# Inverse of the 16x16 blocks by columns' contributions, and two scale-and-shift steps on ScalarE, in a one-core RWKV and HGRN kernel

## Chip, cores and metric

The kernel runs on one core of a Trainium2 chip. The metric is the time of one execution in microseconds, measured on the device; before the change it is 2753.27 us (median of three runs). TensorE multiplies, VectorE and ScalarE do the element-wise work, POOL (GpSimd) and SP (SyncE) here mostly start transfers.

## The reference, cut to what matters

Two transformer blocks over 256 tokens of width 2048. The change lies in the first, in the RWKV-7 recurrence of 32 heads of 64 (`h` for a head, state 64x64):

```python
w = -softplus(-(w0 + tanh(xw @ w1) @ w2)) - 0.5
decay = exp(-exp(w))
a = sigmoid(a0 + (xa @ a1) @ a2)
kk = heads(k * k_k); kk = kk * rsqrt(max(sum(kk * kk), 1e-24))
k = k * (1 + (a - 1) * k_a)
# for each token t, with a_vec = -kk, b_vec = kk * a:
sa = state @ a_t
state = state * w_t + sa b_t^T + v_t k_t^T
y_t = state @ r_t
```

## The kernel before

The recurrence is computed by chunks of 64 tokens. Inside a chunk the tokens depend on each other through a triangular 64x64 matrix, of which the kernel needs the inverse. It inverts the sixteen-wide diagonal blocks on VectorE and joins them with matmuls on TensorE (`s2`, levels `lev16` and `lev32`).

`jit` walks over eight groups of four heads. For each group TensorE makes the products k and v with float32 weights that are split into two parts, `hi` by ScalarE (L183) and `lo` by VectorE (L184), so that each product is three matmuls (`feat_p`, L1043 to L1045). Between these matmuls pieces of three generators are placed by hand: `s0` of the group itself (operands of the recurrence), `s1` of the group before (scores, inverse, transposes) and `s2` of the one before that (joining, the chain over four chunks, output norm). The lists `SLOT0`, `SLOT1`, `SLOT2` give the step j, 0 to 63 (one step for every three matmuls), from which a piece may be issued. Nothing reorders instructions afterwards: each engine takes its own in the order in which the code issues them, and waits where an operand is not ready. A fourth stream, `s3`, multiplies blocks of another weight (`ab<-in_adat`, 512 KB each) on VectorE at L507; it has one buffer, so that SP starts the next transfer only when L507 has read the last, and SP's queue has the weight transfers (`raw`) behind it. After the eighth group `wo` makes the output product, with the last group's `s1` and `s2` beside it; it needs `yhl`, splits of the recurrence's result by ScalarE (L287) and VectorE (L288).

The lines that the change and the prediction touch:

- `s0`, second piece: `sw` is the tanh of the decay's logit (tile `zw`). L1064 turns it into the sigmoid (0.5 x + 0.5); L1067 scans it into C (two instructions); ScalarE makes exp of it twice (L1068, L1070), and the square of `kkr` (L1076). TensorE sums the squares (L1079).
- `s0`, fourth piece: VectorE bounds the sum (L1080), ScalarE makes its inverse root by Ln and Exp (L1082, L1083), VectorE makes (ta - 1) * 0.5 k_a into `kb` from the tanh `ta` (tile `za`), half a group at a time (L1087), then (that + 1) * k (L1090). Later pieces: L1093, L1094, L1099 (into C again) and L1104.
- `s1`: TensorE's L1127 needs C of L1099; L1141 needs `LA` (L1118, L1119) and `kb`. POOL writes the scores `Aa` to device memory and loads the diagonal blocks as `G`, [64, 16, 16]: 64 blocks, one a partition. L1170 to L1182 are the inverse; five `yield`s cut it into six pieces. Then POOL stores P and its transpose and reloads them as `Pm`, `Tm`.
- `s2`: for each chunk c, TensorE makes `ch` (L1246), ScalarE copies it to `U` (L1249), TensorE multiplies by P (L1253), ScalarE copies to `VA`, `VB` (L1261), TensorE updates the state (L1266), ScalarE scales it (L1271), TensorE adds to the output `yT` (L1275).

`half` holds 0.5 w0, 0.5 a0 and 0.5 k_a, made once at L907.

Of the kernel before, what the change touches and what calls it, by code (L numbers as in the profile page):

```python
# [13 lines left out]
AF = mybir.ActivationFunctionType  # L14
ALU = mybir.AluOpType
AX = mybir.AxisListType
# [81 lines left out]
class Kern:  # L98
# [790 lines left out]
    def scan_pools(self, st):  # L889
        tc, nc = self.tc, self.nc  # L890
        self.sp = st.enter_context(tc.tile_pool(name="sc", bufs=1))
        z = self.T([64, 8, 64], "Tm")
        nc.vector.memset(z[:], 0.0)
        self.img = {}
        for i in range(2):
            for n in "PT":
                t = self.img[n, i] = self.dr.tile([1, 8 * CQ], F32, name=f"img{n}{i}")
                for hd in range(2):
                    nc.sync.dma_start(out=self.rows(t, hd), in_=z[:])
        self.Ep = self.T([128, 8, 65], "Ep")  # L900
        nc.vector.memset(self.Ep[:, :, 0:1], 1.0)
        self.scanm = self.sp.tile([128, 256], BF16, name="scanm")
        nc.vector.memset(self.scanm[:], 1.0)
        nc.vector.memset(self.scanm[:, 0:256:64], 0.0)
        self.half = self.T([128, 3, 16], "half")
        for i, n in enumerate(("w0", "a0", "k_a")):
            nc.vector.tensor_scalar(out=self.half[:, i, :], in0=self.v(n, 0, 16), scalar1=0.5, scalar2=None,  # L907
                                    op0=ALU.mult)

    def rows(self, t, hd):  # L910

# [6 lines left out]
    def T(self, shape, tag, bufs=1):  # L918
        return self.sp.tile(list(shape), F32, tag=tag, bufs=bufs, name=tag)
# [130 lines left out]
    def s0(self, g):  # L1050
        nc, f = self.nc, self.gr[g]
        T = self.T
        at = iter(self.SLOT0)
        c8 = lambda t: t.rearrange("p f (c t) -> p (f c) t", c=4)
        fl = lambda t: t.rearrange("p f t -> p (f t)")
        bc = lambda v: v.unsqueeze(2).broadcast_to([128, 2, S])
        vec2 = lambda n: self.v(n, 2 * g, 2)
        yield next(at)
        while self.kdone < g - 1:
            assert self.step("s1")  # L1060
        Ep = self.Ep
        sw, ta = f["w"], f["a"]

        nc.vector.tensor_scalar(out=sw, in0=sw, scalar1=0.5, scalar2=0.5, op0=ALU.mult, op1=ALU.add)  # L1064
        C = T([128, 2, S], "C")
        for i in range(2):
            nc.vector.tensor_tensor_scan(C[:, i, :], self.scanm[:], sw[:, i, :], 0.0, op0=ALU.mult, op1=ALU.add)  # L1067
        nc.scalar.activation(out=Ep[:, :, 1:65], in_=c8(C[:]), func=AF.Exp, scale=-KAPPA)  # L1068
        Em = sw
        nc.scalar.activation(out=Em, in_=C, func=AF.Exp, scale=KAPPA)  # L1070
        yield next(at)

        kkr = f["kkr"] = T([128, 2, S], "kkr")
        nc.vector.tensor_tensor(out=kkr, in0=f["k"], in1=bc(vec2("k_k")), op=ALU.mult)
        rn = rk = f["rk"] = C
        nc.scalar.activation(out=C, in_=kkr, func=AF.Square)  # L1076
        yield next(at)
        p = self.misc((128, 2, S))
        nc.tensor.matmul(fl(p[:]), lhsT=self.c("bones"), rhs=fl(C[:]), start=True, stop=True)  # L1079
        nc.vector.tensor_scalar(out=rn, in0=p[:], scalar1=1e-24, scalar2=None, op0=ALU.max)  # L1080
        self.lnset()
        nc.scalar.activation(out=rn, in_=rn, func=AF.Ln, scale=65536.0)  # L1082
        nc.scalar.activation(out=rn, in_=rn, func=AF.Exp, scale=-0.5, bias=self.b8)  # L1083

        kb = f["kb"] = T([128, 8, 128], "kb")
        for i in range(2):
            nc.vector.tensor_scalar(out=kb[:, i * 4:i * 4 + 4, 64:128],  # L1087
                                    in0=ta[:, i, :].rearrange("p (c t) -> p c t", c=4), scalar1=-1.0,
                                    scalar2=self.half[:, 2, 2 * g + i:2 * g + i + 1], op0=ALU.add, op1=ALU.mult)
        nc.vector.scalar_tensor_tensor(out=kb[:, :, 64:128], in0=kb[:, :, 64:128], scalar=1.0, in1=c8(f["k"][:]),  # L1090
                                       op0=ALU.add, op1=ALU.mult)
        yield next(at)
        nc.vector.tensor_tensor(out=kkr, in0=rn, in1=kkr, op=ALU.mult)  # L1093
        nc.vector.scalar_tensor_tensor(out=kb[:, :, 0:64], in0=c8(ta[:]), scalar=1.0, in1=c8(kkr[:]), op0=ALU.add,  # L1094
                                       op1=ALU.mult)
        yield next(at)
        r = self.r[:, 2 * g:2 * g + 2, :]
        for i in range(2):
            nc.vector.scalar_tensor_tensor(out=rk[:, i, :].rearrange("p (c t) -> p c t", c=4),  # L1099
                                           in0=r[:, i, :].rearrange("p (c t) -> p c t", c=4),  # L1100
                                           scalar=self.v("r_k", 2 * g + i), in1=kb[:, i * 4:i * 4 + 4, 64:128],
                                           op0=ALU.mult, op1=ALU.mult)
        kb4 = kb[:].rearrange("p c (j t) -> p c j t", j=2)
        nc.vector.tensor_tensor(out=kb4, in0=kb4, in1=c8(Em[:]).unsqueeze(2).broadcast_to([128, 8, 2, 64]),  # L1104
                                op=ALU.mult)
        yield next(at)

    def s1(self, g):
        nc, f = self.nc, self.gr[g]
# [4 lines left out]
        Ep, kb, kkr = self.Ep, f["kb"], f["kkr"]  # L1114
# [5 lines left out]
                                       op0=ALU.mult, op1=ALU.mult)  # L1120
# [5 lines left out]
        p = self.misc((128, 2, S))  # L1126
# [7 lines left out]
        for i in range(2):  # L1134
            for hd, L in ((0, LA), (1, LB)):
# [3 lines left out]
                p = self.misc((128, 4, 128))  # L1139
                for c in range(4):  # L1140
# [5 lines left out]
                                        op=ALU.mult)  # L1146
                nc.vector.tensor_tensor(out=L[os, cs, :], in0=p[64:128], in1=mb(slice(64, 128), slice(0, 128)),
                                        op=ALU.mult)
# [7 lines left out]
        for i in range(2):  # L1156
            cs = slice(i * 4, i * 4 + 4)
            p = self.misc((128, 4, 128))
# [7 lines left out]
        G = T([64, 16, 16], "G")  # L1166
# [3 lines left out]
        P = T([64, 16, 16], "PG")  # L1170
        tmp = T([64, 256], "tG")
        nc.vector.memset(P[:], 0.0)
        nc.vector.memset(P[:].rearrange("p a b -> p (a b)")[:, 0:256:17], 1.0)
        for t in range(1, 16):
            tv = tmp[:, 0:t * t].rearrange("p (a b) -> p a b", a=t)
            nc.vector.tensor_tensor(out=tv, in0=P[:, 0:t, 0:t], in1=G[:, 0:t, t].unsqueeze(1).broadcast_to([64, t, t]),
                                    op=ALU.mult)
            nc.vector.tensor_reduce(out=P[:, 0:t, t], in_=tv, axis=AX.X, op=ALU.add)
            if t in (4, 7, 9, 11, 13):
                yield next(at)  # L1180
        Tt = T([64, 16, 16], "tG")
        nc.vector.tensor_copy(out=Tt, in_=P[:].rearrange("p a b -> p b a"))  # L1182
# [12 lines left out]
        p = self.misc((128, 2, 2, 128))  # L1195
# [710 lines left out]
```

## Time and profile before

| | us |
|---|---|
| median of 3 runs (2752.15 to 2753.98) | 2753.27 |
| the profiled execution's own time | 2759.31 |
| its span, first to last instruction | 2757.5 |
| TensorE busy | 2608.1 (95%) |
| VectorE busy | 1775.8 (64%) |
| ScalarE busy | 1346.5 (49%) |
| the change's stage, `jit` and `wo` | about 221 to 790 of the span |

The profile is of one execution, whose time is 6 us above the median. Busy TensorE is the sum of its matmuls' times; the ends of pipelined matmuls are modelled. L12 is line 12 of the kernel; a row names an engine, a line, the tile written and the tiles read. Wait rows say which engine waited for whose result. Times in the timeline count from the start of the span.

### The profile page before, as it was taken

The numbers are of one execution on the slowest core, as the hardware profiler recorded it, in microseconds if no ns is written. First come the engines' busy times: TensorE is split into PE (matmuls) and PEld (weight loads), VectorE is DVE, ScalarE is ACT, GpSimd is POOL, SyncE is SP. The second block draws the span as 40 slices with busy tenths as digits, with TensorE's granted clock in tenths as the row PEclk, the third lists the DMA queues.
The fourth block names the chain that finished last, engine by engine and source line by source line (L and its number), as shares of the span: only waits on it lengthen the run. The fifth ranks groups of instructions, "written<-read, shape, count | busy, mean of one in ns | idle before, by whom it ended". The sixth has DMA issues, their size and how long they took to land.

```text
span 2757.5 us, 47818 instructions
## 1 busy us (share of the span) xinstructions
PE 2608.1 (95%) x19345; PEld 2377.1 (86%) x19345; DVE 1775.8 (64%) x2845; ACT 1346.5 (49%) x2206; POOL 61.6 (2%) x101
## 2 busy tenths in 40 slices
PE   6997999998879999999999989999989999999998
PEld 5997788886559999999888789998789999988887
DVE  5977888887567786666555556665554444555555
ACT  3245565664355444444444555655454444444444
POOL 0000111110000000000000000000000000000000
PEclk8999999999889999999999999999999999999999
DMA  8946555556656775555555544443535555556555
GB/s 326 389 145 200 191 191 185 192 182 205 223 193 240 271 268 187 183 183 184 176 194 194 176 155 145 139 139 122 192 131 184 183 183 183 183 191 194 195 192 159
DMA packets 151516, 534.13 MB, mean 194 GB/s; under 512 B 21376, under 2 KB 21760, under 8 KB 150272
## 3 DMA queue, kind: packets, MB, share of 16 engines
q1 hardware_dynamic: 146640, 515.36, 55.7%
q0 software_dynamic: 4368, 13.64, 1.9%
q8 instruction: 151, 2.47, 0.4%
q10 hardware_dynamic: 288, 2.10, 0.2%
q14 instruction: 69, 0.57, 0.1%
HBM read 524.73 MB, written 6.29 MB: 193 GB/s over the span
## 4 chain that ended last, share of the span: by engine, by line
PE 82%; DVE 6%; ACT 6%; DMA 5%; issue 2%; SPq 0%; DVEq 0%; ACTq 0%; POOLq 0%
PE ta L353 7%; PE ta L354 7%; PE ta L352 7%; PE f L276 6%; PE f L274 6%; PE f L275 6%; PE u L276 4%; PE u L275 4%; PE u L274 4%; PE m L1043 3%; PE m L1044 3%; PE m L1045 3%; DMA scratch<-in_adat 2%; PE r L776 2%; DVE spl L184 1%
## 5 line engine op out<-in xcount | busy, mean ns | idle before, releaser
L184 DVE TENSOR_TENSOR spl<-raw,spl 128x1024 fp32r<-128x1024 f32 x748 | 913.1, 1221 | 778.0 <-ACT spl L183 773.6
L183 ACT CAST spl<-raw 128x1024 fp32r<-128x1024 f32 x748 | 782.0, 1046 | 856.8 <-PE ta L354 307.2
L276 PE MATMUL f<-yhl,spl 128*128 128x256 f32 x1376 | 389.5, 283 | 0.4 <-DVE spl L184 0.4
L274 PE MATMUL f<-yhl,spl 128*128 128x256 f32 x1376 | 389.8, 283 | 0.0
L275 PE MATMUL f<-yhl,spl 128*128 128x256 f32 x1376 | 389.4, 283 | 0.0
L352 PE MATMUL ta<-spl,shl 128*128 128x512 f32 x832 | 324.6, 390 | 3.4 <-ACT shl L287 3.4
L353 PE MATMUL ta<-spl,shl 128*128 128x512 f32 x832 | 324.5, 390 | 1.5 <-DVE spl L184 1.5
L354 PE MATMUL ta<-spl,shl 128*128 128x512 f32 x832 | 324.4, 390 | 0.0
L274 PE MATMUL u<-hl,spl 128*128 128x256 f32 x1024 | 289.9, 283 | 0.0
L276 PE MATMUL u<-hl,spl 128*128 128x256 f32 x1024 | 289.8, 283 | 0.0
L275 PE MATMUL u<-hl,spl 128*128 128x256 f32 x1024 | 289.8, 283 | 0.0
L276 PEld LDWEIGHTS f<-yhl,spl 128*128 128x128 f32 x1376 | 264.2, 192 | 0.6 <-DVE spl L184 0.6
L275 PEld LDWEIGHTS f<-yhl,spl 128*128 128x128 f32 x1376 | 264.2, 192 | 0.0
L274 PEld LDWEIGHTS f<-yhl,spl 128*128 128x128 f32 x1376 | 264.2, 192 | 0.0
L1043 PE MATMUL m<-hl,spl 128*128 128x256 f32 x672 | 199.6, 297 | 0.0
L274 PEld LDWEIGHTS u<-hl,spl 128*128 128x128 f32 x1024 | 196.6, 192 | 0.0
L275 PEld LDWEIGHTS u<-hl,spl 128*128 128x128 f32 x1024 | 196.6, 192 | 0.0
L276 PEld LDWEIGHTS u<-hl,spl 128*128 128x128 f32 x1024 | 196.6, 192 | 0.0
L1044 PE MATMUL m<-hl,spl 128*128 128x256 f32 x672 | 189.9, 283 | 0.0
L1045 PE MATMUL m<-hl,spl 128*128 128x256 f32 x672 | 189.8, 282 | 0.0
L352 PEld LDWEIGHTS ta<-spl,shl 128*128 128x128 f32 x832 | 156.6, 188 | 36.6 <-ACT shl L287 3.8
L353 PEld LDWEIGHTS ta<-spl,shl 128*128 128x128 f32 x832 | 156.6, 188 | 34.5 <-DVE spl L184 2.1
(422 smaller groups left out, 4809.8 us busy)
## 6 DMA issues: line engine op xcount, KB each, us to landing
raw<-in_ffn_in SPq DMA_DIRECT2D x172, 512.0 KB, 4.7
raw<-in_w_up SPq DMA_DIRECT2D x128, 512.0 KB, 3.7
raw<-in_w_down SPq DMA_DIRECT2D x128, 512.0 KB, 4.0
raw<-in_ffn_out SPq DMA_DIRECT2D x86, 512.0 KB, 3.8
raw<-in_w_in SPq DMA_DIRECT2D x84, 512.0 KB, 3.7
raw<-in_w_rkv SPq DMA_DIRECT2D x76, 512.0 KB, 4.5
scratch<-in_adat SPq DMA_DIRECT2D x66, 512.0 KB, 5.9
ada<-in_ada SPq DMA_DIRECT2D x64, 512.0 KB, 6.7
```

Source lines behind the costliest of these rows:

```text
L183: self.nc.scalar.copy(out=hi[:, :n], in_=t[:, :n])
L184: self.nc.vector.tensor_tensor(out=lo[:, :n], in0=t[:, :n], in1=hi[:, :n].bitcast(F32), op=ALU.subtract)
L274: nc.tensor.matmul(out, lhsT=hi[:, w], rhs=xhl[:, 0, kc, :], start=(kc == 0), stop=False)
L275: nc.tensor.matmul(out, lhsT=hi[:, w], rhs=xhl[:, 1, kc, :], start=False, stop=False)
L276: nc.tensor.matmul(out, lhsT=lo[:, w], rhs=xhl[:, 0, kc, :], start=False, stop=(kc == KD - 1))
L352: nc.tensor.matmul(o, lhsT=shl[0][:, t0], rhs=hi[:, w], start=first, stop=False)
L353: nc.tensor.matmul(o, lhsT=shl[0][:, t0], rhs=lo[:, w], start=False, stop=False)
L354: nc.tensor.matmul(o, lhsT=shl[1][:, t0], rhs=hi[:, w], start=False, stop=last)
L776: nc.tensor.matmul(out, lhsT=wd[:, w], rhs=xt[:, g % 2, max(0, min(3, ft - 9)), kc % 2, :], start=False, stop=e)
L1043: nc.tensor.matmul(out, lhsT=hi[:, w], rhs=xhl[:, 0, kc, :], start=(kc == 0), stop=False)
L1044: nc.tensor.matmul(out, lhsT=hi[:, w], rhs=xhl[:, 1, kc, :], start=False, stop=False)
L1045: nc.tensor.matmul(out, lhsT=lo[:, w], rhs=xhl[:, 0, kc, :], start=False, stop=(kc == KD - 1))
```

## The change

1. The inverse is reordered. Before, column t of P was made at once: a product of P's first t columns with column t of G (t x t elements) and a sum over the inner axis. Now column t, when it is done, is multiplied by row t of G and added to all later columns: (t+1) x (15-t) elements, a product and a sum, for t = 1 to 13, with a copy ahead and one fused step for t = 14. There are 28 instructions in place of 30 between the memsets and the transposing copy, and the five `yield`s stand after t = 3, 5, 7, 9 and 12 in place of 4, 7, 9, 11 and 13; how the pieces run together follows below.
2. L1064 is an activation (Copy, scale 0.5, bias 0.5) on ScalarE.
3. L1087 is an activation (Identity, scale 0.5 k_a, bias -0.5 k_a) on ScalarE, L1088 in the changed file; `half` gets a fourth row, -0.5 k_a.

```diff
--- before.py
+++ after.py
@@ -902,10 +902,10 @@
         self.scanm = self.sp.tile([128, 256], BF16, name="scanm")
         nc.vector.memset(self.scanm[:], 1.0)
         nc.vector.memset(self.scanm[:, 0:256:64], 0.0)
-        self.half = self.T([128, 3, 16], "half")
-        for i, n in enumerate(("w0", "a0", "k_a")):
-            nc.vector.tensor_scalar(out=self.half[:, i, :], in0=self.v(n, 0, 16), scalar1=0.5, scalar2=None,
-                                    op0=ALU.mult)
+        self.half = self.T([128, 4, 16], "half")
+        for i, n in enumerate(("w0", "a0", "k_a", "k_a")):
+            nc.vector.tensor_scalar(out=self.half[:, i, :], in0=self.v(n, 0, 16), scalar1=-0.5 if i == 3 else 0.5,
+                                    scalar2=None, op0=ALU.mult)
 
     def rows(self, t, hd):
 
@@ -1061,7 +1061,7 @@
         Ep = self.Ep
         sw, ta = f["w"], f["a"]
 
-        nc.vector.tensor_scalar(out=sw, in0=sw, scalar1=0.5, scalar2=0.5, op0=ALU.mult, op1=ALU.add)
+        nc.scalar.activation(out=sw, in_=sw, func=AF.Copy, scale=0.5, bias=0.5)
         C = T([128, 2, S], "C")
         for i in range(2):
             nc.vector.tensor_tensor_scan(C[:, i, :], self.scanm[:], sw[:, i, :], 0.0, op0=ALU.mult, op1=ALU.add)
@@ -1084,9 +1084,9 @@
 
         kb = f["kb"] = T([128, 8, 128], "kb")
         for i in range(2):
-            nc.vector.tensor_scalar(out=kb[:, i * 4:i * 4 + 4, 64:128],
-                                    in0=ta[:, i, :].rearrange("p (c t) -> p c t", c=4), scalar1=-1.0,
-                                    scalar2=self.half[:, 2, 2 * g + i:2 * g + i + 1], op0=ALU.add, op1=ALU.mult)
+            ka = [self.half[:, j, 2 * g + i:2 * g + i + 1] for j in (2, 3)]
+            nc.scalar.activation(out=kb[:, i * 4:i * 4 + 4, 64:128], in_=ta[:, i, :].rearrange("p (c t) -> p c t", c=4),
+                                 func=AF.Identity, scale=ka[0], bias=ka[1])
         nc.vector.scalar_tensor_tensor(out=kb[:, :, 64:128], in0=kb[:, :, 64:128], scalar=1.0, in1=c8(f["k"][:]),
                                        op0=ALU.add, op1=ALU.mult)
         yield next(at)
@@ -1171,12 +1171,19 @@
         tmp = T([64, 256], "tG")
         nc.vector.memset(P[:], 0.0)
         nc.vector.memset(P[:].rearrange("p a b -> p (a b)")[:, 0:256:17], 1.0)
-        for t in range(1, 16):
-            tv = tmp[:, 0:t * t].rearrange("p (a b) -> p a b", a=t)
-            nc.vector.tensor_tensor(out=tv, in0=P[:, 0:t, 0:t], in1=G[:, 0:t, t].unsqueeze(1).broadcast_to([64, t, t]),
-                                    op=ALU.mult)
-            nc.vector.tensor_reduce(out=P[:, 0:t, t], in_=tv, axis=AX.X, op=ALU.add)
-            if t in (4, 7, 9, 11, 13):
+        nc.vector.tensor_copy(out=P[:, 0, 1:16], in_=G[:, 0, 1:16])
+        for t in range(1, 15):
+
+            n, m = t + 1, 15 - t
+            if m > 1:
+                tv = tmp[:, 0:n * m].rearrange("p (a b) -> p a b", a=n)
+                nc.vector.tensor_tensor(out=tv, in0=P[:, 0:n, t:t + 1].broadcast_to([64, n, m]),
+                                        in1=G[:, t, n:16].unsqueeze(1).broadcast_to([64, n, m]), op=ALU.mult)
+                nc.vector.tensor_tensor(out=P[:, 0:n, n:16], in0=tv, in1=P[:, 0:n, n:16], op=ALU.add)
+            else:
+                nc.vector.scalar_tensor_tensor(out=P[:, 0:n, 15], in0=P[:, 0:n, t], scalar=G[:, t, 15:16],
+                                               in1=P[:, 0:n, 15], op0=ALU.mult, op1=ALU.add)
+            if t in (3, 5, 7, 9, 12):
                 yield next(at)
         Tt = T([64, 16, 16], "tG")
         nc.vector.tensor_copy(out=Tt, in_=P[:].rearrange("p a b -> p b a"))
```

Lines behind the inverse are 7 higher in the changed file (L1249 is L1256, L1261 is L1268, L1271 is L1278, L1275 is L1282).

ScalarE's order in group 3, second piece of `s0`, between two chunks of `s2` (`Ep`, `zw` and `C` belong to `s0`, `VA`, `VB`, `U` to the chain). Before:

```order
L1271 ACTIVATE VA<-ch_3615,ecl 64x64 x2
L1271 ACTIVATE VB<-ch_3615,ecl 64x64 x2
L1068 ACTIVATE Ep<-C 128x8x64
L1070 ACTIVATE zw<-C 128x512
L1076 ACTIVATE C<-kkr 128x512
L1249 COPY U<-ch_3750 128x128
```

and now:

```order
L1278 ACTIVATE VA<-ch_3611,ecl 64x64 x2
L1278 ACTIVATE VB<-ch_3611,ecl 64x64 x2
L1064 ACTIVATE zw<-zw 128x512
L1068 ACTIVATE Ep<-C 128x8x64
L1070 ACTIVATE zw<-C 128x512
L1076 ACTIVATE C<-kkr 128x512
L1256 COPY U<-ch_3744 128x128
```

The halving of `zw` stands behind both scalings of VB and ahead of L1068; VectorE's L1067 needs its result.

VectorE's order in the same group, fourth piece of `s0`, with the end of the inverse ahead of it. Before:

```order
L1176 TENSOR_TENSOR tG<-PG,G 64x225
L1178 TENSOR_REDUCE PG<-tG 64x15
L1182 COPY tG<-PG 64x256
L184 TENSOR_TENSOR spl_3828<-raw_3681,spl_3827 128x1024
L1080 TENSOR_SCALAR C<-mi_3841 128x512
L1087 TENSOR_SCALAR kb<-za,half 128x4x64 x2
L1090 SCALAR_TENSOR_TENSOR kb<-kb,k 128x8x64
L507 SCALAR_TENSOR_TENSOR ab,asum<-ab 128x1024
L1093 TENSOR_TENSOR kkr<-C,kkr 128x512
```

and now:

```order
L1180 TENSOR_TENSOR tG<-PG,G 64x28
L1182 TENSOR_TENSOR PG<-tG,PG 64x14x2
L1184 SCALAR_TENSOR_TENSOR PG<-PG,G 64x15
L1189 COPY tG<-PG 64x256
L184 TENSOR_TENSOR spl_3823<-raw_3675,spl_3822 128x1024
L1080 TENSOR_SCALAR C<-mi_3836 128x512
L1090 SCALAR_TENSOR_TENSOR kb<-kb,k 128x8x64
L507 SCALAR_TENSOR_TENSOR ab,asum<-ab 128x1024
L1093 TENSOR_TENSOR kkr<-C,kkr 128x512
```

and ScalarE's at the same place, before:

```order
L1249 COPY U<-ch_3834 128x128
L291 ACT_TABLE_LOAD
L1082 ACTIVATE C<-C 128x512
L1083 ACTIVATE C<-C,sm 128x512
L1261 COPY VA<-ch_3834 64x2x64
L1261 COPY VB<-ch_3834 64x2x64
```

and now:

```order
L1256 COPY U<-ch_3829 128x128
L291 ACT_TABLE_LOAD
L1082 ACTIVATE C<-C 128x512
L1083 ACTIVATE C<-C,sm 128x512
L1088 ACTIVATE kb<-za,half 128x4x64 x2
L1268 COPY VA<-ch_3829 64x2x64
L1268 COPY VB<-ch_3829 64x2x64
```

L1087 has left VectorE. L1090 follows L1080 at once and takes the `kb` that ScalarE makes behind Ln and Exp and ahead of `VA` and `VB`.

VectorE's order in the inverse's middle pieces, group 3, before:

```order
L1176 TENSOR_TENSOR tG<-PG,G 64x100
L1178 TENSOR_REDUCE PG<-tG 64x10
L1176 TENSOR_TENSOR tG<-PG,G 64x121
L1178 TENSOR_REDUCE PG<-tG 64x11
L1176 TENSOR_TENSOR tG<-PG,G 64x144
L1178 TENSOR_REDUCE PG<-tG 64x12
L1176 TENSOR_TENSOR tG<-PG,G 64x169
L1178 TENSOR_REDUCE PG<-tG 64x13
```

and now:

```order
L1180 TENSOR_TENSOR tG<-PG,G 64x63
L1182 TENSOR_TENSOR PG<-tG,PG 64x9x7
L1180 TENSOR_TENSOR tG<-PG,G 64x60
L1182 TENSOR_TENSOR PG<-tG,PG 64x10x6
L1180 TENSOR_TENSOR tG<-PG,G 64x55
L1182 TENSOR_TENSOR PG<-tG,PG 64x11x5
L1180 TENSOR_TENSOR tG<-PG,G 64x48
L1182 TENSOR_TENSOR PG<-tG,PG 64x12x4
L1180 TENSOR_TENSOR tG<-PG,G 64x39
L1182 TENSOR_TENSOR PG<-tG,PG 64x13x3
```

Between the same neighbours (L1074 ahead, a split behind) stand t = 8 to 12 in place of t = 10 to 13.

## Rows read from the trace of the kernel before

**Rows 1.** Table by stretch: busy us (x instructions), granted clock, DMA share, GB/s.

```profile
262.00:304.00 42.00, 30.62 (x273) 27.21 (x271) 38.85 (x77) 17.75 (x27) 5.61 (x9) 0.88 0.65 217
...
365.00:425.00 60.00, 58.26 (x655) 49.55 (x653) 53.36 (x101) 36.04 (x73) 8.53 (x13) 1.00 0.58 195
```

**Rows 2.** TensorE's waits, 365 to 425 us: us in total, times, longest.

```profile
PE ch L1260 <- ACT VA L1261: 0.8, 2, 0.4
...
PE mi L1141 <- DVE LA L1119: 0.5, 1, 0.5
```

**Rows 3.** VectorE, groups by line, 220 to 700 us: busy us, mean ns | idle.

```profile
L1064 DVE TENSOR_SCALAR zw<-zw 128x512 f32<-128x512 f32 x8 | 3.4, 422 | 0.0
...
L1087 DVE TENSOR_SCALAR kb<-za,half 128x256 f32<-128x256 f32 x16 | 5.1, 359 | 0.0
...
L1176 DVE TENSOR_TENSOR tG<-PG,G 64x1 f32<-64x1 f32 (+14 forms) x120 | 35.5, 296 | 12.1 <-DMA G<-au 9.0
...
L1178 DVE TENSOR_REDUCE PG<-tG 64x1 f32<-64x1 f32 (+14 forms) x120 | 27.9, 232 | 4.1
...
L1176 DVE TENSOR_TENSOR tG<-PG,G 64x64 f32<-64x64 f32 x8 | 2.0, 254 | 0.0
...
L1178 DVE TENSOR_REDUCE PG<-tG 64x8 f32<-64x64 f32 x8 | 1.7, 214 | 0.3
```

**Rows 4.** ScalarE, groups by line and form, whole run or 220 to 700 us.

```profile
L1070 ACT ACTIVATE zw<-C 128x512 f32<-128x512 f32 x8 | 4.9, 613 | 0.0
...
L999 ACT ACTIVATE za<-za,half 128x256 f32<-128x256 f32 x16 | 6.7, 480 | 0.0
...
L339 ACT ACTIVATE hb<-xp,Bf,Af 128x128 f32<-128x128 f32 x32 | 11.7, 462 | 2.2 <-PE xp L403 2.2
```

**Rows 5.** Timeline of group 3, second piece: start us, us, engine, line.

```profile
382.99 0.51 ACT L1271 ACTIVATE VB<-ch,ecl 64x64 f32<-64x64 f32 x2
...
383.07 1.27 DVE L1067 TENSOR_TENSOR_SCAN C<-scanm,zw 128x256 f32<-128x256 bf16 x2
...
384.38 0.63 ACT L1068 ACTIVATE Ep<-C 128x512 f32<-128x512 f32 x1 [0.88 <-DVE C L1067]
...
386.22 0.27 ACT L1249 COPY U<-ch 128x128 f32<-128x128 f32 x1
...
386.71 0.45 PE L1253 MATMUL ch<-U,Pm 64*64 64x64 f32 x8
```

**Rows 6.** Timeline of group 3, fourth piece.

```profile
394.69 0.72 ACT L1083 ACTIVATE C<-C,sm 128x512 f32<-128x512 f32 x1
...
394.70 0.69 DVE L1090 SCALAR_TENSOR_TENSOR kb<-kb,k 128x512 f32<-128x512 f32 x1
...
395.59 0.26 ACT L1261 COPY VB<-ch 64x128 f32<-64x128 f32 x1
...
396.08 0.27 PE L1275 MATMUL yT<-Aq,VA 64*64 64x64 f32 x1
```

**Rows 7.** VectorE's timeline, ends of groups 2 and 3.

```profile
346.54 1.23 DVE L507 SCALAR_TENSOR_TENSOR ab<-ab 128x1024 f32<-128x1024 f32 x1 [1.15 <-DMA ab<-in_adat]
...
405.56 1.23 DVE L184 TENSOR_TENSOR spl<-raw,spl 128x1024 fp32r<-128x1024 f32 x1 [0.44 <-ACT spl L183]
```

**Rows 8.** TensorE's timeline in the output product.

```profile
632.11 0.79 PE L354 MATMUL wo<-spl,yhl 128*128 128x512 f32 x1 [3.73 <-DVE yhl L288]
...
690.58 0.50 PE L354 MATMUL wo<-spl,yhl 128*128 128x512 f32 x1 [1.17 <-DVE yhl L288]
...
699.96 0.51 PE L354 MATMUL wo<-spl,yhl 128*128 128x512 f32 x1 [1.44 <-DVE yhl L288]
```

**Rows 9.** TensorE's timeline in groups 0 and 1.

```profile
242.06 1.33 PE L1127 MATMUL mi<-C,cst 128*128 128x512 f32 x2 [4.47 <-DVE C L1099]
...
272.64 0.58 PE L1045 MATMUL pv<-mx,spl 128*128 128x256 f32 x1 [5.95 <-DVE spl L184]
...
291.05 2.04 PE L1127 MATMUL mi<-C,cst 128*128 128x512 f32 x2 [4.59 <-DVE C L1099]
```

## The prediction

> **What bounds the kernel now.** I read the stage table first. In the steady part of the recurrence (365 to 425 us) TensorE is busy 58.26 of 60 us while VectorE has 53.36 and ScalarE 36.04 [rows 1]: TensorE sets the pace, and all its waits together are under 2 us. [...] Next I read what TensorE waits for in a steady group: `ch` L1260 for ScalarE's copy of VA (0.4 us each) and L1141 for VectorE's `LA` (0.5) [rows 2]. These waits are short because every piece sits in a hand-made slot; the reader should see that the order leaves little room, not much idle time to win.
>
> **The prices.** VectorE loses 0.42 us (L1064) and a pair at 0.36 us each (L1087), 1.14 us a group [rows 3]. The old inverse is 35.5 + 27.9 us over eight groups, 7.9 us each [rows 3]. The new one has 26 products and sums of 28 to 64 elements, a copy and a last fused step. The strided 64x64 product took 0.254 us [rows 3]; that bounds each of the 26 above, and the 0.214 us of the eight-row sum, whose input is as long, bounds it below [rows 3]. I take 0.235 (the operands are partly strided, as in the product) and 0.15 each for the two small ones: 6.4 us, saving 1.5, with 1.0 and 2.0 as ends. On that row the product is slow: 0.254 us for 64 elements. [...] The measured row is the form that is replaced, so I keep it.
>
> On ScalarE a Copy of 128x512 with scale and bias does not occur, but another activation of that length with constants does: L1070, 0.613 us [rows 4]. I take 0.61; L1068, of the same length, took 0.63 [rows 5], and the shorter L999 bounds it below. The two Identity steps have a scale and a bias per partition: L999 with one such operand takes 0.480 us at 128x256, L339 with two 0.462 us at half that length [rows 4]. Both are below the new form, so one is over 0.48; twice L339 is an upper end, 0.92. I take 0.56 each, 1.0 us for the pair with a small overlap. ScalarE's spare time hides these 1.6 us as work. It does not hide where they stand in the queue, and that is the sum. The fourth 128x16 row of `half` runs once, ahead of the stage, while VectorE is about to wait for ScalarE's first split; uncovered it would cost less than one L1087, 0.36 us.
>
> **Term 1, the scan waits for ScalarE.** In group 3 ScalarE ends VB (L1271) at 383.50, VectorE started the scan at 383.07, ScalarE the exponentials (L1068) at 384.38, then `U` at 386.22 to 386.49, and TensorE takes U at 386.71 [rows 5]. In the new order the halving step stands behind VB and ahead of L1068, so the scan cannot start before 383.5 + 0.61 + 0.05 = 384.17, 1.1 us later. L1068, L1070, L1076 and U follow one behind the other on ScalarE: U ends at about 387.6. TensorE, which is in order, reaches L1253 at 386.71 and waits 0.9 us, and the rest of the group is late with it. Both ends hang on TensorE's own earlier products, so this repeats: the other groups from 2 to 7 have the scan earlier and U with more room, and come out alike. 6 x 0.9 = **+5.4**.
>
> **Term 2, kb in front of VA and VB.** The pair stands behind L1083 on ScalarE (end 395.41) and ahead of the copies whose second ends at 395.85; TensorE uses them at 396.08 [rows 6]. The pair puts 1.0 us in front of a room of 0.2 us. The shorter inverse brings L1080 forward by some 0.3 us against TensorE, which leaves 0.5 us; two of the six groups have 0.3 us more room. 6 x 0.4 = **+2.4**.
>
> **Term 3, VectorE's queue behind kb.** L1090 started at 394.70, beside ScalarE's logarithm and exponential [rows 6]. Now it waits for kb, which ScalarE makes only after L1083, and all of VectorE's queue stands behind it: L507 and with it the next `ab` transfer on SP's queue (and the weight transfer issued behind that), L1093 to L1104, the weight split, `LA`. L1083 itself moves by 0.6 (TensorE's 0.9 less the 0.3 of the inverse), so L1090 starts near 395.4 + 0.6 + 1.0 = 397.0, 2.3 us later; TensorE is by then 1.3 us late (terms 1 and 2), so VectorE is 1.0 us behind it. The weight splits bear that, since each is made while the product before the one that needs it runs. In most groups the room behind is nearly enough (the split ahead of `LA` waits 0.44 us for ScalarE [rows 7], and the step before it a little): 0.2 us at L1141 in four groups. In group 2 it is not: L507 waits for its transfer, 1.15 us, and nothing is slack from there to L1141 [rows 7], so 1.3 us. Into the output product the chain through the last `ab` transfer ends the 3.73 us wait for `yhl` [rows 8]: 1.4 us more. 0.8 + 1.3 + 1.4 = **+3.5**.
>
> **Term 4, the first two groups.** TensorE waits 4.47 us at L1127 for VectorE's L1099, which stands behind L1090; then 5.95 us for a split, then again 4.59 us at L1127 [rows 9]. By group 3's rows kb holds L1090 for (395.41 - 394.70) + 1.0 + 0.1 = 1.8 us; here nothing shifts L1083, and the whole chain of VectorE and `ab` transfers goes with it. The halving step saved ahead of it does not help in group 0, since there a weight transfer holds VectorE's split. The 5.95 us wait lies at the end of the same chain, so the 1.8 stays. In group 1 the halving and the inverse give back 0.4 + 1.5, and kb takes 1.8 again. **+1.8**.
>
> **Term 5, the last inverse.** It stands in the output product, with `yhl` splits behind it for which TensorE waits 1.17 and 1.44 us [rows 8]. **-1.5**.
>
> **Sum.** 5.4 + 2.4 + 3.5 + 1.8 - 1.5 = +11.6 us. The profiled execution took 2759.31 us (span 2757.5, 1.8 around it), 6.0 above the median of 2753.27; 2759.3 + 11.6 = 2770.9, so the median goes to 2764.9, 0.42% slower. About 0.2%, 5.5 us, is what a measurement of this kernel tells from no change.
>
> **Rivals.**
> *A, only net engine work counts (same).* TensorE's order has more room than the five rows show, and the change costs the price difference: (0.61 - 0.42) + (1.0 - 0.72) = 0.47 us in eight groups, 3.8 us: 2757.1. For it: every wait in rows 2 is under half a microsecond and groups differ. Against it: L1253 reads U 0.2 us after it is ready, and 1.1 us does not fit. [...] Chance 0.17.
> *B, VectorE's relief pays (faster).* The place is 221 to 304 and 684 to 700 us, where VectorE's queue is what TensorE waits for [rows 1, 8, 9]. Two groups lose 1.14 us each, the inverse gives 2.0 in group 1 and 2.6 in the output product: 7.5 us, 2745.8. It decides if kb is ready no later than VectorE's end of L1080 plus 0.7 us and if U stays in time, that is, if ScalarE runs these steps before the logarithm; the order printed above puts them behind it. Chance 0.05.
> *C, the clock falls too (much slower).* If the new waits bring the steady groups under the upper level for some 4 us each, as in 262 to 304 us, six groups add about 12 us: 2777. Against it: the waits that go with 0.88 are 4.6 and 5.95 us long [rows 1, 9], and the new ones are 0.9. Chance 0.08.
> *Forecast*, all five terms near their size: 0.70.
>
> **The numbers.** The forecast case spans 2759 to 2771: terms 2 and 3 may half vanish (-3), term 1 may lose a group or two (-2), the inverse and ScalarE's pair at their ends move terms 4 and 5 by 2, and each `ab` transfer may land 1 to 2 us later (+3). The range takes in A's upper half and part of C: 2756 to 2773, leaving B, A's lower part and most of C out, about 0.2. Faster by over 0.2%: B, 0.05. Within: A and the foot of the forecast, 0.18. Slower: 0.77.
>
> **What would show it.** In the new profile TensorE should wait about 0.9 us for ScalarE's U once in each of groups 2 to 7, and 0.3 to 0.5 us for VB before `yT`; VectorE should show idle time ended by ScalarE's `zw` L1064 (1 to 2.7 us) and kb L1088 (near 2 us) in all eight groups; the wait at the first L1127 should be near 6.3 us, and the inverse near 6.4 us a group. The forecast is wrong if U is in time (term 1 falls), if L1090's wait is under 1 us (terms 3 and 4), or if the inverse falls below 5 us and the output product gains more than 3.

## The result and the profile after

| | us |
|---|---|
| changed kernel, median of 4 executions (2767.62 to 2777.36) | 2773.41 |
| before, median on the same chip | 2753.62 |
| ratio | 1.0067, 95% interval 1.0051 to 1.0083 |
| the profiled execution's own time, and its span | 2777.36, 2775.6 |

The kernel is slower by 0.67%, where 0.42% was forecast: the ratio times 2753.27 is 2771.7 us, near the top of the range; the median itself lies 0.4 us above it. (The ratio is not the quotient of the two medians, 1.0072, which lies inside its interval.) A second measurement of the same kernel (below) gave 1.0075.

The page after: VectorE lost 25 us of work, ScalarE gained 12.5, and TensorE, which sets the time, shows more busy time for the same products.

```profile
span 2775.6 us, 47799 instructions
...
PE 2620.8 (94%) x19345; PEld 2386.6 (86%) x19345; DVE 1750.9 (63%) x2806; ACT 1359.0 (49%) x2230; POOL 61.3 (2%) x101
```

The first place to look is TensorE's waits, 200 to 800 us of the changed kernel (us in total, times, longest):

```profile
PE ch L1267 <- ACT VA L1268: 7.1, 16, 0.9
PE mi L1127 <- DVE C L1099: 5.6, 1, 5.6
PE ch L1260 <- ACT U L1256: 5.2, 6, 0.9
PE mi L1127 <- ACT spl L183: 5.0, 1, 5.0
...
PE pv L1045 <- DVE spl L184: 4.3, 1, 4.3
...
PE mi L1141 <- DVE LA L1119: 3.6, 5, 1.3
...
PE yT L1282 <- ACT VA L1268: 0.5, 3, 0.2
```

The rows for VA, `LA` and U in the same view of the kernel before:

```profile
PE ch L1260 <- ACT VA L1261: 6.1, 16, 0.4
...
PE mi L1141 <- DVE LA L1119: 2.6, 6, 0.5
...
PE ch L1253 <- ACT U L1249: 0.2, 1, 0.2
```

The third row is new: six waits of 0.87 us for U, where the trace before had one of 0.24. For `LA` TensorE now waits up to 1.3 us instead of 0.5. The row of VA grew too: in groups 2 and 4 TensorE waits 0.86 us for VA (at 334.34 and 449.55), 2 us behind its wait for U, where the longest before was 0.4; no term of the prediction has these two. Why U is late stands in ScalarE's timeline of group 3 (start us, us, engine, line), to be read beside [rows 5]:

```profile
386.07 0.51 ACT L1278 ACTIVATE VB<-ch,ecl 64x64 f32<-64x64 f32 x2
386.60 0.63 ACT L1064 ACTIVATE zw<-zw 128x512 f32<-128x512 f32 x1
388.58 0.63 ACT L1068 ACTIVATE Ep<-C 128x512 f32<-128x512 f32 x1 [1.34 <-DVE C L1067]
389.12 0.61 ACT L1070 ACTIVATE zw<-C 128x512 f32<-128x512 f32 x1
389.76 0.63 ACT L1076 ACTIVATE C<-kkr 128x512 f32<-128x512 f32 x1
390.42 0.27 ACT L1256 COPY U<-ch 128x128 f32<-128x128 f32 x1
```

ScalarE halves `zw` only when VB is done, then idles 1.34 us while VectorE scans, and U is the fourth instruction after that. On VectorE the two moved steps come back as idle time (groups by line, 220 to 715 us: busy us, mean ns | idle, and its releaser):

```profile
L1182 DVE TENSOR_TENSOR PG<-tG,PG 64x28 f32<-64x28 f32 (+6 forms) x104 | 21.1, 203 | 3.6
L1180 DVE TENSOR_TENSOR tG<-PG,G 64x28 f32<-64x28 f32 (+6 forms) x104 | 21.0, 202 | 2.8
...
L1067 DVE TENSOR_TENSOR_SCAN C<-scanm,zw 128x256 f32<-128x256 bf16 x16 | 10.2, 678 | 11.2 <-ACT zw L1064 11.2
...
L1090 DVE SCALAR_TENSOR_TENSOR kb<-kb,k 128x512 f32<-128x512 f32 x8 | 5.5, 692 | 19.5 <-ACT kb L1088 19.5
...
L1184 DVE SCALAR_TENSOR_TENSOR PG<-PG,G 64x15 f32<-64x15 f32 x8 | 1.9, 238 | 0.3
...
L1174 DVE COPY PG<-G 64x15 f32<-64x15 f32 x8 | 1.3, 164 | 8.8 <-DMA G<-au 8.7
```

L1090 waits 2.44 us for kb in each of the eight groups; in group 3 ScalarE makes kb right behind L1083 (timelines of ScalarE and VectorE, beside [rows 6]):

```profile
398.45 0.72 ACT L1083 ACTIVATE C<-C,sm 128x512 f32<-128x512 f32 x1
399.07 1.08 ACT L1088 ACTIVATE kb<-za,half 128x256 f32<-128x256 f32 x2
400.19 0.69 DVE L1090 SCALAR_TENSOR_TENSOR kb<-kb,k 128x512 f32<-128x512 f32 x1 [2.44 <-ACT kb L1088]
```

What the waits do not explain is in the table by stretch (us, TensorE busy, its loads, VectorE, ScalarE, POOL, then the granted clock):

```profile
332.00:336.00 4.00, 2.85 (x39) 2.04 (x39) 3.54 (x10) 2.80 (x7) 0.00 (x0) 1.00 0.00 0
336.00:340.00 4.00, 4.00 (x24) 3.13 (x20) 1.76 (x3) 2.83 (x7) 1.68 (x2) 0.57 0.88 290
340.00:344.00 4.00, 4.00 (x44) 3.45 (x43) 1.26 (x2) 3.28 (x7) 2.38 (x4) 1.00 0.17 48
...
485.00:545.00 60.00, 57.34 (x597) 48.18 (x593) 46.32 (x90) 36.03 (x72) 6.99 (x11) 0.94 0.51 178
```

Up to 332.29 TensorE had waited for U and up to 334.34 for VA; from about 336 the granted clock is down: 0.57 in the row of 4 us, 1.7 us lost (in rows of 0.5 us it is 1.00 up to 336, 0.50 from 336.5 to 339.5 and 1.00 again from 340). In the kernel before, no 4-us row between 308 and 620 us is under 1.00, and the stretch of the last row reads

```profile
485.00:545.00 60.00, 57.74 (x623) 49.24 (x621) 52.29 (x103) 39.13 (x78) 7.00 (x11) 1.00 0.56 184
```

In the changed kernel falls stand in 336 to 340, 504 to 516 and 588 to 596, the last two behind U at 504.97 and `LA` at 587.17: each behind a wait that the change made or lengthened.

One sum keeps waits and clock apart. A **period** here is the time from TensorE's late U product of group 2 to that of group 7, five groups; the loss to the clock is (1 - granted clock) x 4 us, summed over the 4-us rows in it. It is an upper estimate: it counts low clock also where TensorE waits, and at 0.50 the 128x256 products of the changed kernel start 0.21 us apart (336.54 to 337.82), against 0.12 at 1.00 (388.26 to 389.58), which is less than twice.

| kernel profiled | period, us | over before | lost to the clock | the rest |
|---|---|---|---|---|
| before | 276.5 | | 0 | |
| changed | 291.1 | 14.6 | 6.8 | 7.8 |
| changed, second profile | 294.3 | 17.7 | 10.3 | 7.5 |
| e1 inverse alone | 276.7 | 0.1 | 0 | 0.1 |
| e2 halving alone | 287.8 | 11.2 | 6.8 | 4.4 |
| e3 kb alone | 282.4 | 5.9 | 0 | 5.9 |
| e12 kb alone, second profile | 289.9 | 13.4 | 6.9 | 6.5 |
| e4 kb early | 287.8 | 11.3 | 6.8 | 4.4 |
| e5 halving alone, filler | 282.7 | 6.2 | 0 | 6.2 |
| e6 halving alone, U first | 285.7 | 9.2 | 5.1 | 4.1 |
| e7 e4 with U first | 286.5 | 10.0 | 6.8 | 3.1 |
| e8 inverse and kb early | 277.5 | 0.9 | 0 | 0.9 |
| e9 halving at the tangents | 276.2 | -0.3 | 0 | -0.3 |
| e10 the same, with the inverse | 276.9 | 0.3 | 0 | 0.3 |

For e2 the rest, 4.4 us, is five waits of 0.87; the two longer waits for VA, which e2 has as well, would add 1.0, so the split is good to some 1 us. Of the 18.1 us between the two spans, 0.8 come ahead of this period, 14.6 in it, and 2.7 behind it. Only the period is steady enough to be read so. From its end to the last product of `wo` the kernel before takes 213.0 us and the changed one 215.8, but the changed one's second profile 209.5, and the two profiles of e3's and e12's kernel 208.4 and 217.4: what the change does in the output product these profiles do not resolve.

### The profile page after: what moved, and what is told of

It is laid out like the page before. It is cut to its first block, busy times and chain, and to the rows that moved or that the text cites. A ratio compares the mean times of both kernels' runs of the same rounds, so it can differ in the third digit from the quotient of the medians.

```text
span 2775.6 us, 47799 instructions
## 1 busy us (share of the span) xinstructions
PE 2620.8 (94%) x19345; PEld 2386.6 (86%) x19345; DVE 1750.9 (63%) x2806; ACT 1359.0 (49%) x2230; POOL 61.3 (2%) x101
## 4 chain that ended last, share of the span: by engine, by line
PE 81%; DVE 6%; ACT 6%; DMA 5%; issue 2%; SPq 0%; DVEq 0%; ACTq 0%; POOLq 0%
PE ta L353 7%; PE ta L354 7%; PE ta L352 7%; PE f L276 6%; PE f L274 6%; PE f L275 6%; PE u L276 4%; PE u L275 4%; PE u L274 4%; PE m L1043 3%; PE m L1044 3%; PE m L1045 3%; DVE spl L184 1%; DMA scratch<-in_adat 1%; PE r L776 1%
## 5 line engine op out<-in xcount | busy, mean ns | idle before, releaser
L274 PE MATMUL u<-hl,spl 128*128 128x256 f32 x1024 | 289.9, 283 | 0.0
```

The source lines that it names most:

```text
L274: nc.tensor.matmul(out, lhsT=hi[:, w], rhs=xhl[:, 0, kc, :], start=(kc == 0), stop=False)
```

## The experiments

Ratios are to the kernel before, timed on the same chip. The expectations set three theories against each other. Queue theory: the cost comes from where the new steps stand in ScalarE's queue. Price theory: it is the difference in engine time, wherever they stand. Clock theory: the new waits of TensorE bring its granted clock down as well. The first question was which part costs. Each of e1, e2 and e3 has one part of the printed diff alone.

**e1, the inverse alone** (the last hunk only).

```diff
-        for t in range(1, 16):
...
+        nc.vector.tensor_copy(out=P[:, 0, 1:16], in_=G[:, 0, 1:16])
+        for t in range(1, 15):
...
```

> Only the inverse is changed; both scale-and-shift steps stay on VectorE. Queue theory (the loss comes from where ScalarE's new steps stand): no wait for ScalarE's U or for kb appears, the inverse costs 5.7 us a group instead of 7.9, the steady groups stay at 55.25 us each, and the saving shows only where VectorE is waited for, in group 1 and in the output product: 2749 to 2752 us. Rival (the reordered inverse itself is part of the loss, since its pieces are cut at other places and push the splits behind them): 2755 to 2760 us. Clock theory (the clock falls because of new waits of TensorE): no fall of the granted clock between 308 and 620 us, as before.

Measured: 0.9979 (0.9967 to 0.9991), median 2749.88 us. The inverse gains 5.8 us. The steady groups did not move (table above), so the gain lies ahead of or behind them, as the queue theory said; TensorE's waits for L1099 at L1127 went from 9.1 to 4.5 us in all. How much came where the profile does not tell, since those stretches also differ by 3 and 9 us between the two profiles of e3's and e12's kernel. The rival falls: the new cuts cost nothing net, though in group 0 the wait for `LA` grew from 0.30 to 1.83 us.

**e2, the halving alone** (the L1064 hunk only).

```diff
-        nc.vector.tensor_scalar(out=sw, in0=sw, scalar1=0.5, scalar2=0.5, op0=ALU.mult, op1=ALU.add)
+        nc.scalar.activation(out=sw, in_=sw, func=AF.Copy, scale=0.5, bias=0.5)
```

> Only the halving step of zw is moved to ScalarE. Queue theory: TensorE waits 0.9 us for U once in each of groups 2 to 7, +5.4 us: 2757 to 2760 us without anything else. Price theory (only 0.63 against 0.42 us in eight groups): +1.7, 2755 us. Clock theory: the same waits make the granted clock fall in one to three stretches of the steady groups, 2 to 7 us on top: 2760 to 2766 us in all.

Measured: 1.0031 (1.0020 to 1.0041), 2764.37 us, which is 8.5 us by the ratio. U waits in six groups, 5.2 us in all, and behind five of these six waits the clock falls. Price theory, at 1.7 us, is too small. The fall in group 3, by 4-us rows, behind the wait that ended at 386.82:

```profile
384.00:388.00 4.00, 3.14 (x33) 2.57 (x33) 3.76 (x12) 2.99 (x5) 0.00 (x0) 1.00 0.47 188
388.00:392.00 4.00, 3.65 (x29) 3.08 (x29) 3.90 (x8) 1.54 (x6) 0.00 (x0) 0.65 0.18 44
392.00:396.00 4.00, 4.00 (x39) 3.01 (x39) 3.35 (x7) 3.58 (x5) 1.67 (x2) 0.93 0.81 257
```

**e3 and e12, the kb pair alone** (the hunks of `half` and L1087), measured twice.

```diff
-            nc.vector.tensor_scalar(out=kb[:, i * 4:i * 4 + 4, 64:128],
...
+            nc.scalar.activation(out=kb[:, i * 4:i * 4 + 4, 64:128], in_=ta[:, i, :].rearrange("p (c t) -> p c t", c=4),
+                                 func=AF.Identity, scale=ka[0], bias=ka[1])
```

> Only the kb pair is moved to ScalarE, where it stands behind the logarithm and the exponential. Queue theory: VectorE waits 2.4 us for kb in all eight groups, TensorE pays 1 to 2 us in the first two, some 0.2 at VA and up to 0.9 at LA in the steady ones: +3 to +8, 2756 to 2761 us. Price theory: (1.08 - 0.72) x 8 = +2.9, 2756 us, with no new wait of TensorE. Clock theory: a fall of the clock behind the longer waits for LA, up to 4 us more.

> The kb pair alone on ScalarE, again, for a second profile: the first one showed no fall of the clock between 308 and 620 us and was its fastest execution, 10 us under its median. Clock theory: a profile of median time shows falls of some 5 us and more in the steady groups. Queue theory alone: none, and the waits themselves are longer than in the first. Ratio 1.003 to 1.006.

Measured: 1.0043 (1.0027 to 1.0059), 2770.20 us, and 1.0066 (1.0047 to 1.0084), 2774.81 us. This is the dearest part: 12 and 18 us, over the range of the queue theory (3 to 8 us), and e12's ratio is over its own (1.003 to 1.006). Of the waits, VectorE's 2.44 us for kb in every group came as expected; TensorE's for `LA` reached 1.7 and 2.0 us, where 0.9 was expected. e3's profile is of the fastest of its seven executions (2759.63 us), e12's of the slowest of its four (2779.94). They differ by 20 us, of which 7.5 in the period, and 6.9 of these are the clock, as the clock theory had it; most of the others, 9 us, lie in the output product. In the second profile, `LA` in group 5 (row of TensorE's timeline, then 4-us rows):

```profile
527.62 0.57 PE L1141 MATMUL mi<-LA,kb 64*128 64x128 f32 x3 [1.96 <-DVE LA L1119]
```

```profile
524.00:528.00 4.00, 2.04 (x35) 1.79 (x32) 3.96 (x8) 0.49 (x1) 0.00 (x0) 1.00 0.62 244
528.00:532.00 4.00, 4.00 (x46) 3.55 (x46) 3.97 (x7) 1.97 (x4) 0.00 (x0) 0.51 0.28 93
532.00:536.00 4.00, 4.00 (x47) 3.75 (x44) 2.54 (x5) 0.00 (x0) 0.00 (x0) 0.63 0.45 173
```

In the first the same wait was nearly as long and the clock stayed up, so such a wait need not bring a fall:

```profile
522.17 0.34 PE L1141 MATMUL mi<-LA,kb 64*128 64x128 f32 x1 [1.69 <-DVE LA L1119]
```

```profile
520.00:524.00 4.00, 2.31 (x22) 1.88 (x22) 4.00 (x6) 1.93 (x3) 0.00 (x0) 1.00 0.29 118
524.00:528.00 4.00, 4.00 (x81) 3.80 (x78) 3.83 (x7) 0.53 (x2) 0.00 (x0) 1.00 0.61 222
```

The three parts add to 0.53% with e3's ratio and 0.76% with e12's; the whole change measured 0.67 and 0.75.

The second question was whether the work on ScalarE costs, or its place. **e4, the changed kernel with the kb pair right behind L1064**, where ScalarE idles for the scan.

```diff
         nc.scalar.activation(out=sw, in_=sw, func=AF.Copy, scale=0.5, bias=0.5)
+        kb = f["kb"] = T([128, 8, 128], "kb")
+        for i in range(2):
...
-        kb = f["kb"] = T([128, 8, 128], "kb")
-        for i in range(2):
...
```

> The changed kernel with the kb pair moved on ScalarE to right behind the halving step, where ScalarE waits 1.3 us for the scan. Queue theory: the wait of VectorE for kb goes, and with it those of TensorE for VA and the long ones for LA; the wait for U (0.9 us in six groups) stays: 2754 to 2759 us. If the price on ScalarE were what counts: as the changed kernel, 2770 us. Clock theory: some of the falls of the clock stay, since the waits for U stay: 2758 to 2765 us.

Measured: 1.0019 (1.0008 to 1.0031), 2761.82 us. Moving two instructions in ScalarE's queue takes back 0.48 of the 0.67%; VectorE's waits for kb and the long ones for `LA` are gone, U's stay (TensorE's waits, 200 to 800 us), and so do three falls of the clock in the period.

```profile
PE ch L1260 <- ACT U L1256: 5.2, 6, 0.9
...
PE mi L1141 <- DVE LA L1119: 2.7, 6, 0.6
```

**e9, the halving alone, right behind the tangents**, and **e10, the same with the new inverse.**

```diff
+                    if n == "a":
+                        nc.scalar.activation(out=f["w"], in_=f["w"], func=AF.Copy, scale=0.5, bias=0.5)
                 self.deferred.append(ev)
...
-        nc.vector.tensor_scalar(out=sw, in0=sw, scalar1=0.5, scalar2=0.5, op0=ALU.mult, op1=ALU.add)
```

> The halving step alone on ScalarE, but right behind the two hyperbolic tangents, some 5 us ahead of VB: the scan on VectorE then waits for nothing on ScalarE, and the stretch between VB and U holds the old work only. Queue theory (the place is what costs): no wait for U, 0.2 us at VA at most; ratio 0.998 to 1.001 against 1.0031 at its old place. Price theory (0.63 on ScalarE for 0.42 on VectorE wherever it stands): 1.0031 again. A third way: the weight split behind the tangents comes 0.6 us later and TensorE waits for it, 1.002 to 1.004.

> The new inverse with the halving step right behind the tangents; the kb pair left on VectorE. Queue theory: the inverse's gain stays and the halving costs nothing, 0.996 to 0.999. Price theory: 0.9979 + 0.0031 = 1.001.

Measured: e9 1.0002 (0.9991 to 1.0013), 2754.45 us; e10 0.9972 (0.9960 to 0.9983), 2749.49 us. The same 0.65 us of ScalarE that cost 0.31% behind VB costs nothing measurable (0.13% at most) some 5 us earlier. In e9's timelines of group 3 the scan starts without a wait, while ScalarE is still at VB, and the first exponential follows 1.0 us behind VB, as in the kernel before (0.88) and not 2.0 us as in the changed one:

```profile
375.37 0.65 ACT L1002 ACTIVATE zw<-zw 128x512 f32<-128x512 f32 x1
...
379.55 0.51 ACT L1272 ACTIVATE VB<-ch,ecl 64x64 f32<-64x64 f32 x2
379.75 1.27 DVE L1068 TENSOR_TENSOR_SCAN C<-scanm,zw 128x256 f32<-128x256 bf16 x2
381.06 0.63 ACT L1069 ACTIVATE Ep<-C 128x512 f32<-128x512 f32 x1 [0.99 <-DVE C L1068]
```

The price theory of the expectation (1.0031 again) falls; 1.7 us for the plain difference in engine time, 0.06%, lies inside e9's interval and is not excluded. e10 beats both kernels; against e1 (0.9979) the difference is inside the intervals.

**e6, the halving alone with U copied ahead of L1070 and L1076**, and **e7, e4 with the same remedy.** The two activations are kept back and issued right behind U's copy.

```diff
-        nc.scalar.activation(out=Em, in_=C, func=AF.Exp, scale=KAPPA)
...
+        def late():
+            nc.scalar.activation(out=Em, in_=C, func=AF.Exp, scale=KAPPA)
+            nc.scalar.activation(out=C, in_=kkr, func=AF.Square)
...
             nc.scalar.copy(out=U, in_=ch[:, :, 0:64])
+            if self.late:
+                self.late()
+                self.late = None
```

> The halving step alone on ScalarE, but in groups 2 to 7 ScalarE copies U right behind the first exponential and runs the second exponential and the square of kkr after it. Queue theory: U comes 1.2 us sooner, the wait of 0.87 us is gone, and with it the falls of the clock behind it: ratio 0.998 to 1.0005. Price theory: the same work stands on ScalarE, so 1.0031 as with the halving alone.

> All three parts of the change, with both remedies: the kb pair right behind the halving step, and U copied ahead of the second exponential and the square. Queue theory: no new wait of TensorE is left, and what VectorE is relieved of (1.1 us a group and 2.2 in the inverse) pays in the first two groups and the output product: ratio 0.994 to 0.998, no worse than the inverse alone (0.998). Price theory: ScalarE's work costs what it costs: 1.0019 as with the kb pair moved alone. Clock theory: no fall between 308 and 620 us.

Both expectations missed: e6 1.0034 (1.0022 to 1.0045), 2762.40 us; e7 1.0008 (0.9999 to 1.0018), 2757.72 us. e6's ratio is the price theory's number, but the profile shows the time in waits and the clock: U is in time, and the wait moved one step on. The copies of VA now stand behind the two activations and a weight split, and TensorE waits for them, 11.0 us in 16 waits (longest 1.8) in place of 7.1 in e2 and 6.1 before. The falls of the clock did not go either: three in the period in e6, four in e7, all behind these waits for VA. ScalarE's timeline of group 3 in e6, and TensorE's next row:

```profile
386.24 0.27 ACT L1256 COPY U<-ch 128x128 f32<-128x128 f32 x1
386.40 0.63 ACT L1078 ACTIVATE zw<-C 128x512 f32<-128x512 f32 x1
387.06 0.63 ACT L1079 ACTIVATE C<-kkr 128x512 f32<-128x512 f32 x1
387.60 1.03 ACT L183 CAST spl<-raw 128x1024 fp32r<-128x1024 f32 x1
388.54 0.25 ACT L1271 COPY VA<-ch 64x128 f32<-64x128 f32 x1
```

```profile
388.84 0.43 PE L1270 MATMUL ch<-VB,cst 64*64 64x128 f32 x2 [0.85 <-ACT VA L1271]
```

From VB to VA ScalarE pauses only for the scan (1.34 us here); in both orders tried, with the halving in this stretch, one of the copies is late. **e8, inverse and early kb pair, halving left on VectorE**:

```diff
         nc.vector.tensor_scalar(out=sw, in0=sw, scalar1=0.5, scalar2=0.5, op0=ALU.mult, op1=ALU.add)
+        kb = f["kb"] = T([128, 8, 128], "kb")
+        for i in range(2):
...
```

> The new inverse, the halving step left on VectorE, the kb pair on ScalarE ahead of the first exponential. Queue theory: the pair delays the exponentials by 0.2 us in groups where the scan comes late and by up to 1.1 where ScalarE did not wait for it; U waits 0.2 to 0.6 us in six groups, +1 to +4 us against the inverse alone; VectorE's relief in the first two groups gives up to 1.4 back: ratio 0.998 to 1.000. If the clock falls behind these waits too: up to 1.002.

Measured: 0.9992 (0.9982 to 1.0002), 2751.64 us, between e1 and before, with no fall of the clock between 308 and 620 us. U waits in one group (0.33 us) and not in six; VA waits 0.81 us in two groups instead. Against e1 the pair gains nothing, though VectorE is relieved of 0.72 us a group; the 0.13% by which e8 stands above e1 is inside the intervals, and about the pair's difference in engine time, (1.08 - 0.72) x 8 = 2.9 us or 0.10%.

The third question was the clock. **e11, the changed kernel again.** No edit.

> The changed kernel as it is, for a second profile and a time on the chip of these runs. Clock theory: again several stretches of lowered clock between 308 and 620 us, each within 8 us behind one of the new waits (U 0.87 us, LA over 1 us), 4 to 9 us in all; ratio 1.005 to 1.008. If the first profile's falls were chance: none or one, at the same ratio.

Measured: 1.0075 (1.0061 to 1.0089), 2775.59 us. Five falls in place of three, 10.3 us in the period, in groups 3 and 4 as well as in 2, 5 and 6. In the four profiles of the changed kernel (two), e2 and e12, sixteen falls stand between 308 and 620 us, and each begins within some 5 us behind a wait of 0.87 to 2.0 us for U or `LA` that the kernel before did not have at that length; in groups 2 and 4 a wait of 0.86 us for VA lies between. Each fall costs 1.7 us or, in four of them, 3.4 (by the 4-us rows).

**e5, e2 with a filler**: four products of zeros into `yT` ahead of the product that waits for U.

```diff
+            if c == 2 and g < 6:
+                for _ in range(4):
+                    nc.tensor.matmul(yT[:].rearrange("p f c t -> p (f c t)"), lhsT=self.zb[:],
+                                     rhs=self.zb[:].unsqueeze(1).broadcast_to([128, 4, 128]), start=False, stop=False)
```

> The kernel with the halving step alone on ScalarE, plus four products of zeros that TensorE adds to yT just ahead of the product that waits 0.87 us for U, in groups 2 to 7 (24 products of 128x512, some 0.2 us each). TensorE's engine time grows by some 5 us, all of it inside the wait, and U comes no sooner. Clock theory (a gap of this length on TensorE makes the granted clock fall behind it, 1.4 to 1.9 us a group): the falls behind U go, and the kernel gets faster than with the halving alone by 4 to 9 us: ratio to before 1.000 to 1.002 (halving alone: 1.0031). Queue theory alone (the wait is the whole cost): no gain, 1.0031 to 1.0045. If the clock minds what the products compute rather than that they run, zeros change nothing.

Measured: 1.0029 (1.0019 to 1.0039), 2760.36 us. In the profile all falls behind U are gone, and the filler takes 1.04 us where the wait took 0.87:

```profile
328.71 1.04 PE L1253 MATMUL yT<-zb 128*128 128x512 bf16 x4
329.74 0.45 PE L1257 MATMUL ch<-U,Pm 64*64 64x64 f32 x8
```

```profile
384.00:388.00 4.00, 3.90 (x37) 2.76 (x36) 3.76 (x11) 3.06 (x6) 0.00 (x0) 1.00 0.47 180
388.00:392.00 4.00, 3.75 (x39) 2.97 (x40) 3.90 (x7) 2.65 (x8) 0.00 (x0) 1.00 0.20 69
392.00:396.00 4.00, 4.00 (x39) 3.34 (x37) 3.93 (x8) 3.20 (x6) 1.67 (x2) 1.00 0.76 229
```

The profiled period is 5.0 us shorter than e2's although U comes no sooner; its rest, 6.2 us, is five fillers of 1.04 and the two longer waits for VA, which stay at 0.86 us and have no fall behind them here. The timed ratio, though, did not move beyond its interval (1.0031 to 1.0029, where 1.000 to 1.002 was expected). The profiled execution is the fastest of e5's eleven, 4.1 us under their median, and e3 and e12 show that one kernel can have a profile without falls and one with three. So that busy products in the wait keep the clock up is seen in one execution and not shown; the times do not bear it out.

## Why the prediction came out as it did

The direction and the mechanism were right: both steps cost by where they stand in ScalarE's queue (e4, e9). Rival A's price difference (3.8 us) would be about a fifth of the loss; e9 and e8 leave room for it but do not show it. The size, +11.6 against some +18, failed in one step, the clock. That the time still fell inside the range is in part luck: the terms ended at 2771 us, the range went to 2773 because it took in part of rival C, and 2771.7 lies between.

- **Term 1** (0.9 x 6 = 5.4): six waits, 5.2 us. Right. The halving itself takes 638 ns, against 0.61 us taken.
- **Term 2** (0.4 x 6 = 2.4): 0.5 us in the changed kernel. Mis-sized: without the halving, in e3, the same wait is 1.7 us, so TensorE, late through U, seems to reach VA when the kb pair is nearly out of the way.
- **Term 3** (L1090 2.3 us late, +3.5): L1090 waits 2.44. The waits for `LA` grew from 2.6 to 3.6 us in all, in other groups than the one named: group 2 waits 0.49 (0.45 before), group 6 the longest, 1.33 (at 587.17). Mis-sized: in the period that is 1.3 us more, against 2.1. The 1.4 us in the output product can't be checked, for the reason given under the table.
- **Term 4** (+1.8): not there, as far as these waits show. The first wait at L1127 is 5.61 us, not 6.3, and of the two behind it one grew (4.59 to 5.0) and one shrank (5.95 to 4.3), so the three sum to 14.9 as against 15.0 [rows 9]. The 5.95 did not hand the 1.8 us on, as the term had it.
- **Term 5** (-1.5) and the inverse: e1 gains 5.8 us by its ratio (2.5 to 9.1 by the interval), against 3.0 in the terms (1.5 in group 1, 1.5 in the output product). The instructions of lines 1174 to 1184 take (21.1 + 21.0 + 1.9 + 1.3) / 8 = 5.66 us a group, not 6.4. Here the measured row of the old form misled: the 64x64 product takes 217 ns in the new order, against 254 [rows 3].
- **The kb pair**: 586 ns an instruction, 1.08 us the pair, against 0.56 and 1.0 taken.
- **Rival C**, the clock, is the step that failed. It was given 0.08 because "the waits that go with 0.88 are 4.6 and 5.95 us long, and the new ones are 0.9". The profiles show falls behind waits of 0.87 us. The rival's 12 us are an estimate, six times 4 us at half the clock; the kernel before shows the half, 1.00 from 262 to 270 us and 0.50 from 271 to 276 (rows of 1 us). Over the five groups of the period terms 1 to 3 came to 8.6 us (4.5 + 2.0 + 2.1), and 7.8 and 7.5 were found beside the clock, which agrees better than the parts do: U 4.4 us, `LA` 1.3, the waits before `yT` at most 0.5 instead of 2.0, and 1.0 for VA that no term had. The clock added 6.8 and 10.3, of which the forecast had none and C some 10 for five groups. The excess over the forecast (some 7 us) is thus about this one item, as far as profiled executions show it; for the timed ones, which have no rows, it is inferred, and the filler's ratio does not confirm it. Why one such wait is followed by a fall and the next is not stays open.
- **Rival B** (its parts, 2.28 + 2.0 + 2.6, add to 6.9 us and not 7.5) asked that ScalarE run these steps early enough. e10 does that for the halving and is faster, 0.9972, but by the inverse; the halving itself is worth nothing measurable in either engine (e9).

## What to carry to other kernels

Where one engine is 97% busy and in order, moving work to an engine with half its time free is decided by the instructions ahead of and behind the new place, not by that free time: here the same 0.65 us cost 0.31% behind VB and nothing measurable behind the tangents. Look for a place where the operand is ready and no copy that TensorE waits for stands behind. When a new wait on TensorE can't be avoided, add to its length a possible fall of the clock, here 1.7 or 3.4 us each in the profiles, and do not take the longest waits of the old trace as the only ones that bring it.

## What was not expected of the hardware

- The granted clock fell, as far as 0.50 (changed kernel, 508 to 512 us) and 0.51 (e12, 528 to 532), behind TensorE waits of only 0.85 to 2.0 us, behind five of six in e2, and not behind all of them (three of the U waits of the changed kernel in the period, 1.69 us for `LA` in e3 and 1.33 us for it in e10 had no fall). No fall stands between 308 and 620 us in the profiles of the kernel before, e1, e8 and e9, which have no such wait there.
- Two profiles of one kernel differ by 7.5 us in five groups, 6.9 of it through the clock (e3, e12), and by 9 us in the output product behind them.
- The old inverse's 64x64 product took 254 ns and the new one 217, with the same element count and other strides of the operands; whether the strides are the cause was not tried.
